# Eight weight tiles of a Trainium2 kernel begin at eight different places modulo 512 bytes

## The chip, the cores and the metric

The kernel runs on one core of a Trainium2 chip. A core has TensorE (matmuls, listed as PE, with its loads of the stationary operand as PEld), VectorE (DVE), ScalarE (ACT), GpSimd (POOL) and SyncE (SP, which only issues transfers here), an on-chip memory of 128 partitions from which these engines read (SBUF), the matmuls' accumulators (PSUM), and DMA queues between memory off the chip and SBUF. The metric is the device time of one execution in microseconds. A difference of 0.2% or more, some 2.2 us, can be told from no change.

## The reference, cut to what matters

Two layers of a transformer on a sequence of 512 with a width of 1024, in float32. Each layer projects the normalised input, runs two groups of attention heads, projects back, and then applies a dense network with a squared ReLU, whose hidden width is 4096:

```python
for l in range(DEPTH):
    h = rmsnorm(x, attn_norm[l])
    proj = jnp.einsum('bsd,de->bse', h, w_in[l])
    ...                        # stick-breaking heads and differential heads
    x = x + jnp.einsum('bse,ed->bsd', mixed, w_o[l])
    h = rmsnorm(x, mlp_norm[l])
    u = jnp.square(jax.nn.relu(jnp.einsum('bsd,df->bsf', h, w_ff1[l])))
    x = x + jnp.einsum('bsf,fd->bsd', u, w_ff2[l])
return rmsnorm(x, final_norm)
```

## The kernel before, in words

**Three products for one.** A matrix product in float32 is made of three matmuls on rounded operands. An operand a is split into hi, its rounding, and lo = a - hi, the rest; the helper `three` (lines 300, 301, 302) adds hi·hi, hi·lo and lo·hi in one accumulator. So every block of weights that arrives from memory is first split: ScalarE writes the rounded weights (`whi`, line 117, in `round`), VectorE writes the rest (`wlo`, line 133, in `split_part`).

**Units and turns.** All weights are cut into units of 128 partitions by 1024 elements (4096 bytes a partition), listed in `_UNITS` in the order in which TensorE uses them. The class `_Weights` loads, splits and hands out units. A pool named `wspl` holds two pairs of `whi` and `wlo` throughout; while the feed-forward stage of a layer runs, a second pool `f2` adds two more pairs. That makes the eight tiles. `spot` gives each unit its turn k (0 and 1 in `wspl`, 2 and 3 in `f2`), `owner` remembers which unit had the turn before, and `do_split` writes a unit's split into the program only behind the use of the unit that had its turn. Which of a pool's two buffers a tile gets is up to the pool: before the change `whi` and `wlo` are tags with two buffers each, and the tile framework, which also orders the instructions of each engine by its own planning, takes a buffer that is free.

**Where the split tiles are read.** In the attention stage a projection's unit is TensorE's loaded operand (`block`), or its streamed one (`values_of`, `all_values`), in matmuls of 512 or 256 columns. In the feed-forward stage the first product of a layer's first group is done by eight blocks of 24 matmuls with 512 columns (tiles named f); the other groups' first products are done by seven forms of 256 columns (`quad_group`, units of the kind s), and the second products by seven forms of 512 columns, in which the split weights stream and the activations Ah and Al are loaded (units of the kind f, into accumulators X, V, W and Y).

**Sources.** A unit's float32 weights arrive by transfers from SyncE in one of three `raw` buffers (`load`, line 110), in a tile of the feed-forward stage named q, waves, norms or first_a to first_c, some of them with a second transfer from GpSimd that adds another block on the way. A raw buffer is loaded again when its unit has been split; transfers of one queue keep their order.

**Places.** Before the change all eight tiles begin at multiples of 512 bytes in their partition, and so do the activations, the sources and the other large tiles. A few small ones and the two tiles named C of the stick-breaking heads, which begin at 352 and 384 modulo 512, don't. Matmuls read slices that begin at multiples of 512 bytes within their tiles.

Of the kernel before, what the change touches and what calls it, by code (L numbers as in the profile page):

```python
# [9 lines left out]
F32 = mybir.dt.float32  # L10
F32R = mybir.dt.float32r
# [6 lines left out]
P = 128  # L18
# [18 lines left out]
MAN = ()  # L37
APART = (("s", 0, 1), ("s", 3, 0), ("s", 3, 1))
_CTX = {}
DLY_R, DLY_D, DLY_S, DLY_Q = 3.5, 10.2, 9.0, 6.0  # L40
TAIL, ATT, DENSE, CAP = 6.0, 53.0, 145.0, 0.1
FORMS = ("11", "x3", "x2", "21", "x1", "x4", "22")
# [51 lines left out]
class _Weights:  # L94
# [24 lines left out]
    def split_part(self, i, a, b):  # L119
        nc = self.nc  # L120
        if i not in self.tiles and i in self.home:
            self.tiles[i] = self.home[i]
        if i not in self.tiles:
            k = self.spot(i)
            self.owner[k] = i
            self.turn = k + 1
            hi = self.pools[k // 2].tile([P, 1024], F32R, tag="whi", name=f"whi{i}")
            lo = self.pools[k // 2].tile([P, 1024], F32R, tag="wlo", name=f"wlo{i}")
            self.tiles[i] = (hi, lo)
        hi, lo = self.tiles[i]  # L130
        raw = self.first if (i, b) == (0, P) else self.raw[i]
        h = self.round(hi[:, a:b], raw[:, a:b])
        self.last = h, nc.vector.tensor_tensor(  # L133
            out=lo[:, a:b], in0=raw[:, a:b], in1=hi[:, a:b].bitcast(F32), op=ALU.subtract)

    def spot(self, i):
        n = 2 * len(self.pools) if _UNITS[i][0] in "1fs" else 2
        return self.turn % n if self.turn < n else 0
# [27 lines left out]
def trunk(ctx, tc, opened, xT, w, w2, w1, gfin, lamv, cos, sin, out):  # L166
    nc = tc.nc
    cp = ctx.enter_context(tc.tile_pool(name="cp", bufs=1))
    wraw = ctx.enter_context(tc.tile_pool(name="wraw", bufs=3))
    wspl = ctx.enter_context(tc.tile_pool(name="wspl", bufs=2))  # L170
    ps = ctx.enter_context(tc.tile_pool(name="ps", bufs=2, space=PSUM))
    dp = ctx.enter_context(tc.tile_pool(name="dp", bufs=1, space=bass.MemoryType.DRAM))

# [4 lines left out]
    def bank(tag, name):  # L178
        if tag == "any":
            tag = ("mm", "s", "s", "mm", "s")[turn[0] % 5]  # L180
            turn[0] += 1
        ring[0] += tag == "s"
        return ps.tile([P, 512], F32, tag=tag, name=name, bufs=banks[tag])

    if MAN:
        ctx.enter_context(tc.manual_schedule(engines={getattr(mybir.EngineType, e) for e in MAN}))
    W = _Weights(nc, w, wraw, wspl)
    cp.tile([P, 32], F32, tag="lead", name="lead")
    begin = cp.tile([P, 192], F32, tag="begin", name="begin")
    g_all, W.first = begin[:, 0:64], begin[:, 64:192]  # L190
    x = cp.tile([P, KC, S], F32, tag="x", name="x")
# [13 lines left out]
    for c in range(KC):  # L205
        nc.sync.dma_start(x[:, c, :], xT[c])
        if c % 2 == 0:
            for i in range(c < 4, 2):
                nc.sync.dma_start(raws[i][:, c * P : (c + 2) * P], w[i][:, c * P : (c + 2) * P])
    W.raw = dict(enumerate(raws))  # L210
    W.loaded = 2
    W.load(3)

# [51 lines left out]

    W.behind = behind

# [42 lines left out]
    def block(name, tag="mm"):  # L310
        pt = bank(tag, name)
        u = W.next("px" if name[0] == "p" else "1")
        for c in range(KC):
# [22 lines left out]
    for l in range(L):  # L336
# [539 lines left out]
        with ExitStack() as fctx:  # L876
            fe = fctx.enter_context(tc.tile_pool(name=f"fe{l}", bufs=1))
            fp = fctx.enter_context(tc.tile_pool(name=f"ff{l}", bufs=1))
            f2 = fctx.enter_context(tc.tile_pool(name=f"f2{l}", bufs=2))
            last = l == L - 1  # L880
            y = {q: (fe if q == (0, 0) else fp).tile([P, 2, 512], F32, tag=f"y{q[0]}{q[1]}", name=f"y{q[0]}{q[1]}_{l}")
                 for q in ((0, 0), (1, 0), (0, 1), (1, 1))}
            def quad(g, q, c):
                return w2[((l * GROUPS + g) * GP // 2 + c) * len(QUADS) + QUADS.index(q)]
# [7 lines left out]
            def fetch(g, form, c):  # L892
                t = W.raw[_INDEX[("f", l, g, form, c)]] = kept[(HOME[form], c)]
                nc.sync.dma_start(t, quad(g, "12" if form == "x3" else form, c))
                if form == "x3":
                    nc.gpsimd.dma_start(t, quad(g, "22", c), accum_op=ALU.add)
# [76 lines left out]
                            then(("f", l, g, "22", c), fetch, g + 1, "21", c)  # L973
            for c in range(GP // 2):
                fetch(0, "11", c)
            W.pools.append(f2)

            if not last:
# [229 lines left out]
            for g in range(GROUPS):  # L1208
# [24 lines left out]
                for form in FORMS2:  # L1233
# [20 lines left out]
                    for n, (c, i, r, part) in enumerate(work):  # L1254
# [3 lines left out]
                        hi, lo = (e[:, :, i, :] for e in sides[c])  # L1258
# [138 lines left out]
```

## Time and profile before

| what | before |
|---|---|
| device time, median of 3 runs | 1121.34 us (1121.09 to 1122.08) |
| profiled execution, device time | 1120.46 us |
| profiled execution, span from first to last instruction | 1118.7 us |
| mean granted TensorE clock | 0.998 |
| TensorE busy | 1111.2 us, 6345 matmuls |
| VectorE busy | 908.3 us |
| ScalarE busy | 689.7 us |
| GpSimd busy | 151.8 us |

The busy times are those of one profiled execution, in which the engines run side by side. A matmul's listed length goes beyond the start of the next, so the distance between starts says how fast TensorE gets on. In the view of stretches each column gives an engine's busy time in the stretch and, in brackets, the number of its instructions. In a group's row the number behind the bar is the group's total, then the mean of one instruction in ns, then the engine's idle time just before, with what ended it.

### The profile page before, as it was taken

Reading aid. Unit: us, or ns where it says so; the run is one execution under the profiler, and the core shown is the slowest. Engines: PE = TensorE matmul, PEld = TensorE weight load, DVE = VectorE, ACT = ScalarE, POOL = GpSimd, SP = SyncE. Lnnn points to the kernel's source line nnn. Section 1 sums busy time; section 2 is a strip of 40 time slices with the busy share of each in tenths; the row PEclk is TensorE's granted clock in tenths of the full one; section 3 lists DMA queues with packets and bytes.
Section 4 is the critical chain, followed back from the end, with each engine's and each line's share of the span. In section 5 each row is a group of like instructions: output and inputs, shape, how many; then the busy total and the mean of one; then the engine's idle time right before and its main releaser. Section 6 shows DMA issues by size and latency. Waiting matters only on the chain.

```text
span 1118.7 us, 17170 instructions
## 1 busy us (share of the span) xinstructions
PE 1111.2 (99%) x6345; PEld 973.8 (87%) x6345; DVE 908.3 (81%) x1333; ACT 689.7 (62%) x1131; POOL 151.8 (14%) x233
## 2 busy tenths in 40 slices
PE   9999999999999999999999999999999999999997
PEld 7889889888899899899878898988888998998986
DVE  7799788898668779779877897897787787797787
ACT  6447767577558457367344576775774584674665
POOL 1001343101001001001000014430011010010010
PEclk9999999999999999999999999999999999999999
DMA  7476353268787678648325654512677886687462
GB/s 256 131 189 187 114 135 110 78 233 218 179 213 183 176 189 189 190 131 213 108 76 152 188 161 128 164 58 76 210 178 184 201 189 177 182 186 207 114 132 95
DMA packets 61044, 181.25 MB, mean 162 GB/s; under 512 B 7456, under 2 KB 8736, under 8 KB 60960
## 3 DMA queue, kind: packets, MB, share of 16 engines
q1 hardware_dynamic: 50160, 141.84, 40.2%
q0 software_dynamic: 10368, 37.75, 19.4%
q8 instruction: 50, 0.82, 0.3%
q10 hardware_dynamic: 432, 0.56, 0.1%
q14 instruction: 34, 0.28, 0.1%
HBM read 150.77 MB, written 4.19 MB: 139 GB/s over the span
## 4 chain that ended last, share of the span: by engine, by line
PE 97%; DVE 1%; issue 1%; ACT 0%; DMA 0%; POOL 0%; POOLq 0%; DVEq 0%; ACTq 0%
PE X L300 9%; PE X L302 9%; PE X L301 9%; PE V L300 4%; PE V L302 4%; PE V L301 4%; PE wo L300 3%; PE wo L301 3%; PE wo L302 3%; PE f L302 3%; PE f L300 3%; PE f L301 3%; PE Y L302 2%; PE Y L300 2%; PE Y L301 2%; PE W L302 1%
## 5 line engine op out<-in xcount | busy, mean ns | idle before, releaser
L117 ACT ACTIVATE whi<-q 128x1024 fp32r<-128x1024 f32 x96 | 101.7, 1059 | 108.5 <-PE X L302 38.0
L133 DVE TENSOR_TENSOR wlo<-q,whi 128x1024 fp32r<-128x1024 f32 x96 | 117.3, 1223 | 46.7 <-ACT whi L117 46.5
L133 DVE TENSOR_TENSOR wlo<-raw,whi 128x1024 fp32r<-128x1024 f32 (+1 forms) x82 | 96.8, 1187 | 6.7 <-ACT whi L117 6.4
L117 ACT ACTIVATE whi<-raw 128x1024 fp32r<-128x1024 f32 (+1 forms) x82 | 80.9, 994 | 33.6 <-issue 17.9
L300 PE MATMUL X<-whi,Ah 128*128 128x512 f32 x248 | 97.7, 394 | 0.0
L301 PE MATMUL X<-wlo,Ah 128*128 128x512 f32 x248 | 96.8, 390 | 0.0
L302 PE MATMUL X<-whi,Al 128*128 128x512 f32 x248 | 96.8, 390 | 0.0
L133 DVE TENSOR_TENSOR wlo<-waves,whi 128x1024 fp32r<-128x1024 f32 x40 | 48.9, 1223 | 16.6 <-ACT whi L117 16.5
L117 ACT ACTIVATE whi<-waves 128x1024 fp32r<-128x1024 f32 x40 | 42.2, 1055 | 29.9 <-PE X L302 18.9
L300 PEld LDWEIGHTS X<-whi,Ah 128*128 128x128 f32 x248 | 46.6, 188 | 11.9 <-DVE y L1121 1.9
L302 PEld LDWEIGHTS X<-whi,Al 128*128 128x128 f32 x248 | 46.6, 188 | 9.8
L300 PE MATMUL X<-hxh,whi 128*128 128x256 f32 x192 | 54.5, 284 | 0.0
L302 PE MATMUL X<-hxh,wlo 128*128 128x256 f32 x192 | 54.4, 284 | 0.0
L302 PE MATMUL X<-h_hi,wlo 128*128 128x256 f32 x192 | 54.4, 284 | 0.0
L301 PE MATMUL X<-h_lo,whi 128*128 128x256 f32 x192 | 54.4, 284 | 0.0
L301 PE MATMUL X<-hxl,whi 128*128 128x256 f32 x192 | 54.4, 284 | 0.0
L301 PEld LDWEIGHTS X<-wlo,Ah 128*128 128x128 f32 x248 | 46.6, 188 | 8.9
L300 PE MATMUL X<-h_hi,whi 128*128 128x256 f32 x192 | 54.4, 283 | 0.0
L300 PE MATMUL f<-h_hi,whi 128*128 128x512 f32 x128 | 50.4, 394 | 0.0
L302 PE MATMUL f<-h_hi,wlo 128*128 128x512 f32 x128 | 50.0, 390 | 0.0
L301 PE MATMUL f<-h_lo,whi 128*128 128x512 f32 x128 | 49.9, 390 | 0.0
L240 DVE TENSOR_TENSOR Al<-x,Ah 128x512 fp32r<-128x512 f32 (+1 forms) x60 | 46.6, 793 | 3.7 <-ACT Ah L239 3.5
(764 smaller groups left out, 3705.4 us busy)
## 6 DMA issues: line engine op xcount, KB each, us to landing
raw<-in_w SPq DMA_DIRECT2D x78, 512.0 KB, 3.6
q<-in_w SPq DMA_DIRECT2D x48, 512.0 KB, 4.4
q<-in_w POOLq DMA_DIRECT2D x48, 512.0 KB, 7.5
waves<-in_w SPq DMA_DIRECT2D x28, 512.0 KB, 4.5
first_a<-in_w SPq DMA_DIRECT2D x12, 512.0 KB, 5.1
first_b<-in_w SPq DMA_DIRECT2D x12, 512.0 KB, 5.3
first_c<-in_w SPq DMA_DIRECT2D x12, 512.0 KB, 4.5
first_b<-in_w POOLq DMA_DIRECT2D x12, 512.0 KB, 6.2
```

The source lines that it names most:

```text
L117: return self.nc.scalar.activation(o, src, AF.Copy)
L133: self.last = h, nc.vector.tensor_tensor(out=lo[:, a:b], in0=raw[:, a:b], in1=hi[:, a:b].bitcast(F32), op=ALU.subtract)
L240: nc.vector.tensor_tensor(out=lo, in0=src, in1=hi.bitcast(F32), op=ALU.subtract)
L300: nc.tensor.matmul(pt, ah, bh, start=first, stop=False, skip_group_check=goes_on),
L301: nc.tensor.matmul(pt, ah, bl, start=False, stop=False, skip_group_check=goes_on),
L302: nc.tensor.matmul(pt, al, bh, start=False, stop=last, skip_group_check=goes_on))
```

## The change

The two buffers of each tag become two tags of one buffer each (`whi0`, `whi1`, `wlo0`, `wlo1`), and a tile takes the one that its turn names. A new function lays out a pool once, when it is opened: it allocates a pad, then a tile, four times, so that the tags stand in the pool in this order with these pads in between; neither the pads nor these first tiles are ever written or read. The first pool's pads sum to 512 bytes; the second pool's sum to 448, and it is the last in its stage. The eight tiles then begin, modulo 512, at 0 and 64 (`whi`, `wlo` of turn 0), 128 and 256 (turn 1), 192 and 320 (turn 2), 384 and 448 (turn 3).

```diff
+PADS = ((0, 64, 64, 128, 256), (192, 128, 64, 64))
...
-            hi = self.pools[k // 2].tile([P, 1024], F32R, tag="whi", name=f"whi{i}")
-            lo = self.pools[k // 2].tile([P, 1024], F32R, tag="wlo", name=f"wlo{i}")
+            hi, lo = (self.half(self.pools[k // 2], n, k % 2, f"{n}{i}") for n in ("whi", "wlo"))
...
+    def half(self, pool, kind, k, name):
+        return pool.tile([P, 1024], F32R, tag=f"{kind}{k}", name=name)
+
+    def lay_out(self, pool, pads):
+        places = [(k, kind) for k in range(2) for kind in ("whi", "wlo")]
+        for n, pad in enumerate(pads):
+            if pad:
+                pool.tile([P, pad // 4], F32, tag=f"pad{n}", name=f"pad{n}")
+            if n < 4:
+                k, kind = places[n]
+                self.half(pool, kind, k, f"place{kind}{k}")
...
-    wspl = ctx.enter_context(tc.tile_pool(name="wspl", bufs=2))
+    wspl = ctx.enter_context(tc.tile_pool(name="wspl", bufs=1))
...
     W = _Weights(nc, w, wraw, wspl)
+    W.lay_out(wspl, PADS[0])
...
-            f2 = fctx.enter_context(tc.tile_pool(name=f"f2{l}", bufs=2))
+            f2 = fctx.enter_context(tc.tile_pool(name=f"f2{l}", bufs=1))
...
+            W.lay_out(f2, PADS[1])
             W.pools.append(f2)
```

## The prediction

> **What bounds the kernel now.** I read the page's totals and the chain that ended last, then the busy time by stretch, then TensorE's order of time in single stretches.
>
> ```profile
> span 1118.7 us, 17170 instructions
> PE 1111.2 (99%) x6345; PEld 973.8 (87%) x6345; DVE 908.3 (81%) x1333; ACT 689.7 (62%) x1131; POOL 151.8 (14%) x233
> PE 97%; DVE 1%; issue 1%; ACT 0%; DMA 0%; POOL 0%; POOLq 0%; DVEq 0%; ACTq 0%
> ```
>
> ```profile
> core 0: us, PE busy (x) PEld busy (x) DVE busy (x) ACT busy (x) POOL busy (x), PEclk, DMA share, GB/s
> 0.00:224.00 224.00, 222.57 (x1208) 190.55 (x1209) 185.92 (x351) 139.55 (x297) 44.08 (x82) 1.00 0.51 150
> 246.00:532.00 286.00, 286.00 (x1734) 256.73 (x1733) 225.32 (x266) 180.86 (x231) 31.73 (x36) 1.00 0.75 192
> ```
>
> TensorE holds 97% of the chain. In the feed-forward stretch (246 to 532 us) it is busy for all 286.00 us at the full granted clock, so a faster or slower split shows only if TensorE has to wait for it, or if TensorE's own reading changes. A matmul's listed duration overlaps the next one; what counts is the distance between starts:
>
> ```profile
> 173.77 0.28 PE L438 MATMUL p0u<-whi,h_hi 128*128 128x256 f32 x1
> ...
> 175.19 0.28 PE L440 MATMUL p0u<-whi,h_lo 128*128 128x256 f32 x1
> ...
> 314.62 0.39 PE L300 MATMUL X<-whi,Ah 128*128 128x512 f32 x1
> ...
> 318.02 0.39 PE L300 MATMUL X<-whi,Ah 128*128 128x512 f32 x1
> ...
> 324.82 0.28 PE L300 MATMUL X<-hxh,whi 128*128 128x256 f32 x1
> ...
> 326.98 0.28 PE L300 MATMUL X<-hxh,whi 128*128 128x256 f32 x1
> ```
>
> From 314.62 to 318.02 there are 15 steps of 512 columns: 226.7 ns each. From 324.82 to 326.98 there are 18 steps of 256 columns: 120.0 ns each. The difference, 106.7 ns for 256 columns, is 0.417 ns a column, and extrapolated to no columns 13.3 ns are left in every step. The rounded weights are the streamed operand in the first stretch and the loaded one in the second, and both leave the same 13.3 ns. In the attention stretch from 173.77 to 175.19 there are 12 steps of 256 columns: 118.3 ns each, a fixed part of 11.7 ns.
>
> **The change, part by part.** Before, every one of the eight tiles (and every large tile) begins at a multiple of 512 bytes. After, whi and wlo of the first pool lie at 0 and 64, then 128 and 256; those of the second at 192 and 320, then 384 and 448.
>
> *Pads and placing tiles.* They are allocated and never written or read: no instruction, no DMA, 0 us. The first pool grows by 512 bytes, so what follows keeps its place modulo 512, and the second pool is the last of its stage. No DMA writes or reads the eight tiles, so transfers keep their places too.
>
> *The splits.* Each unit is rounded on ScalarE (L117) and its rest is taken on VectorE (L133), whose operands now begin at three different places.
>
> ```profile
> L133 DVE TENSOR_TENSOR wlo<-q,whi 128x1024 fp32r<-128x1024 f32 x96 | 117.3, 1223 | 46.7 <-ACT whi L117 46.5
> L117 ACT ACTIVATE whi<-q 128x1024 fp32r<-128x1024 f32 x96 | 101.7, 1059 | 108.5 <-PE X L302 38.0 <-PE V L302 24.7 <-PE Y L302 16.6
> L984 DVE TENSOR_TENSOR x<-x 128x512 f32<-128x512 f32 x48 | 33.1, 689 | 10.2 <-ACT x L1083 9.7
> L984 DVE TENSOR_TENSOR norms<-norms 128x256 f32<-128x256 f32 x16 | 6.8, 422 | 0.1
> L737 POOL TENSOR_TENSOR os<-os,rb 128x512 f32<-128x512 f32 x8 | 10.3, 1289 | 13.5 <-ACT rb L294 13.5
> L578 POOL TENSOR_TENSOR sig0s<-sig0s,C0s 128x512 f32<-128x512 f32 x8 | 9.2, 1146 | 13.3 <-DVE C0s L575 7.7 <-DVE sig0s L571 3.3 <-ACT turned L239 2.3
> ```
>
> VectorE's two-input operation takes 422, 689 and 1223 ns for 256, 512 and 1024 elements: 1.04 ns an element between each pair, a straight line with no extra as it gets longer. The nearest rows with another place are GpSimd's: os and rb both begin at multiples of 512 and take 1289 ns; sig does too, but C begins at 352 or 384 and is read one element further, and the same product takes 1146 ns, 143 ns less. So a place can matter to some engine. Carried over to 1024 elements that is 286 ns a split, the bound on either side. VectorE's own straight line speaks against a gain, so I take 0. At the bound a loss would hardly show either: the feed-forward stretch has units of 12 matmuls (2.72 us), VectorE is busy for 225.32 / 286.00 of that, 2.14 us, and 2.43 us after. Only where the chain leaves TensorE, at the end, does a split stand on it:
>
> ```profile
> 1099.94 1.07 ACT whi L117
> 1101.03 1.23 DVE wlo L133
> 1104.15 1.22 DVE wlo L133
> ```
>
> Two rests at 286 ns are 0.6 us, either way.
>
> *TensorE's reads.* 5388 of the 6345 matmuls (counted in the compiled kernel before) read one of the eight tiles. Half of 1056 such reads of whi in the attention stages and a quarter of 2536 in the feed-forward stages are of the one that stays at place 0; 4226 read a moved one. The only rows of before with an operand off the common place are the transposes that spread a column (rc, at 224 or 256), beside transposes at the common place:
>
> ```profile
> 131.84 0.49 PE L651 MATMUL T0s<-edge,sig0s 128*128 128x128 f32 x3
> 132.16 0.60 PE L293 MATMUL rb_d<-edge,rc 128*128 128x128 f32 x4
> ```
>
> The three starts from 131.84 to 132.16 are 107 ns apart, and the group of four lists 0.60 us where the group of three lists 0.49: one more transpose, 0.11 us more. No difference by place is seen: I take 0. The bounds: the whole fixed part could go, 4226 x 13.3 ns = 56 us; or it moves by what the attention stretch shows it can, 13.3 to 11.7, 1.6 ns x 4226 = 6.8 us, in either direction.
>
> The Trainium skill ("TensorE: Matmul & The Clock Gate", section Back-to-back issue gap) gives a gap of N/2.4 + 2.5 ns at full clock, 215.8 ns for 512 columns and 109.2 for 256. The trace has 226.7 and 120.0, 10.8 to 10.9 more; if the page's gap were the true floor and the surplus all collision, 4226 x 10.8 ns = 46 us would go and the sum would be 1075 us, an estimate from that page. Its page "SBUF — State Buffer" (section Who interferes with whom) says instead that TensorE's two read ports wait on nobody, by which the sum stays; the equal 13.3 ns at both widths, whichever operand is the split tile, agrees.
>
> *Each tile bound to its turn.* The pool gave a unit whichever of its two buffers was free first; now the turn decides. Followed through all units this alters one thing a layer: the fourth block of the first feed-forward product. Its split, the row at 242.91, used the buffer of the first block. Bound to turn 1 it shares with the second block, whose matmuls end at 247.8. This is an added wait of some 5 us.
>
> ```profile
> 242.91 1.05 ACT L117 ACTIVATE whi<-raw 128x1024 fp32r<-128x1024 f32 x1
> 249.17 1.05 ACT L239 ACTIVATE hxh<-x 128x1024 fp32r<-128x1024 f32 x1
> 251.16 1.04 ACT L117 ACTIVATE whi<-raw 128x1024 fp32r<-128x1024 f32 x1
> 250.45 1.22 DVE L240 TENSOR_TENSOR hxl<-x,hxh 128x1024 fp32r<-128x1024 f32 x1
> 251.58 1.28 DVE L240 TENSOR_TENSOR Al<-waves,Ah 128x512 fp32r<-128x512 f32 x2
> 247.57 0.39 PE L302 MATMUL f<-h_hi,wlo 128*128 128x512 f32 x1
> 253.24 0.39 PE L300 MATMUL f<-h_hi,whi 128*128 128x512 f32 x1
> 253.69 0.39 PE L302 MATMUL f<-h_hi,wlo 128*128 128x512 f32 x1
> 243.70 3.34 SPq L110 DMA_DIRECT2D raw<-in_w  x3
> 247.09 1.56 SPq L894 DMA_DIRECT2D q<-in_w  x3
> q<-in_w SPq DMA_DIRECT2D x5, 512.0 KB, 6.6
> q<-in_w POOLq DMA_DIRECT2D x2, 512.0 KB, 9.7
> 274.97 1.06 ACT L117 ACTIVATE whi<-q 128x1024 fp32r<-128x1024 f32 x1
> ```
>
> The block starts at 253.24 and needs its rest at 253.69. Rounding at 249.17 (the first place on ScalarE after the second block's eviction) ends at 250.22, the rest 1.22 us later at 251.4: early by 2.2 us, hidden behind the third block. Behind it on SyncE stand the raw load into the split's source buffer and the q loads of 247.09: from 251.4 they land 6.6 us and, with GpSimd's adding load, another 9.7 us later, at 267.7, and the split that reads them runs at 274.97. Cost 0.
>
> **Sum.** 1120.46 us (profiled execution: span 1118.7 and 1.76 around it) + 0 + 0 + 0 = 1120.5; the median shown, 1121.34, is 0.9 higher, and I give the forecast on that: 1121.3.
>
> **The rivals.** *The fixed part is partly a collision of the weight load with the stream, which different places loosen.* For it: the fixed part is not the same in all stretches (11.7 against 13.3), and GpSimd's two rows. Against: 13.3 ns at both widths and in both roles. By the 1.6 ns it gives 1121.3 - 6.8 = 1114.5; if all went, 1065. The skill's gap, above, is this rival's page.
>
> *The fourth block's split comes late (slower).* If its rounding lands only at 251.16 and its rest stands behind hxl and Al as well (VectorE is busy from 247 to 253 without a gap), it ends at 252.2 + 1.22 + 1.28 + 1.22 = 255.9, 2.2 us after 253.69, in both layers: 1125.7. It decides from the moment when the rest ends after 253.69. For it: VectorE is full there. Against: the split stands ahead of most of that work in program order.
>
> *The new places cost TensorE*, the first rival with its sign turned: 1128.1. Only the spread of the fixed part speaks for it, and the transposes against it.
>
> *The change doesn't do what it says* can only mean that places do not matter; that is the forecast.
>
> **How the numbers follow.** About 0.2% (2.2 us) is what a measurement of this kernel can tell from no change. Forecast: 0.55, its own range 1119.5 to 1123. First rival 0.21, most of it at 1114.5 and at most 0.06 of it below 1111. Late split 0.12, new places costing 0.12. Faster is the first rival, 0.21; slower the two others, 0.24. From 1111 to 1129 all is held but 0.06 below and some 0.06 above, of the costing places at more than the row's 1.6 ns.
>
> **What would show it.** Right: starts stay 226.7 and 120.0 ns apart in the same feed-forward stretches, L133 stays at 1223 and L117 at 1059 ns, the third rounding of the group at 241 to 245 us moves behind 247.9 and no matmul waits at 253. Wrong: another distance between starts for some turns and not for others (first or third rival, by sign), L133 off 1223 by more than 10 ns with the chain leaving TensorE more often, or a gap of TensorE before the fourth block. The prediction as a whole fails if the order of instructions on TensorE or VectorE comes out different far from that block, since I have assumed that it stays.

## The result and the profile after

Before, the time was 1121.21 us in the runs beside the changed kernel (1120.69 to 1122.08). After the change it is **1127.03 us** (1126.45 to 1127.36), a ratio of 1.0051 with a 95% interval of 1.0033 to 1.0068. The kernel became slower by 5.8 us, where no change was forecast. Lines 300 to 302 (`three`) are now 313 to 315, and line 117 is 118.

The page of the changed kernel, its totals and the chain:

```profile
span 1125.4 us, 17171 instructions
PE 1118.0 (99%) x6345; PEld 970.0 (86%) x6345; DVE 909.2 (81%) x1333; ACT 689.3 (61%) x1131; POOL 151.8 (13%) x233
PE 99%; issue 0%; DVE 0%; POOL 0%; ACT 0%; POOLq 0%; DVEq 0%; ACTq 0%
```

TensorE's busy time grew by 6.8 us (1111.2 to 1118.0) and the span by 6.7. VectorE, ScalarE and GpSimd are within 1 us of before. So nothing new is waited for: the same 6345 matmuls take longer. The two stretches shown of before, now:

```profile
core 0: us, PE busy (x) PEld busy (x) DVE busy (x) ACT busy (x) POOL busy (x), PEclk, DMA share, GB/s
0.00:224.00 224.00, 222.63 (x1200) 189.57 (x1201) 184.38 (x348) 139.53 (x297) 44.07 (x82) 1.00 0.51 149
246.00:532.00 286.00, 286.00 (x1729) 253.65 (x1728) 224.23 (x265) 180.64 (x232) 31.70 (x36) 1.00 0.75 192
```

In the same 224 us TensorE gets 1200 matmuls done instead of 1208, and 1729 instead of 1734 in the 286 us of the feed-forward stretch, at an unchanged granted clock of 1.00. In order of time, with the same kinds of steps as before:

```profile
317.76 0.39 PE L313 MATMUL X<-whi,Ah 128*128 128x512 f32 x1
...
321.22 0.39 PE L313 MATMUL X<-whi,Ah 128*128 128x512 f32 x1
...
328.27 0.28 PE L313 MATMUL X<-hxh,whi 128*128 128x256 f32 x1
...
330.06 0.28 PE L313 MATMUL X<-hxh,whi 128*128 128x256 f32 x1
```

Between the first two rows lie 15 steps of 512 columns, 230.7 ns each (226.7 before). Between the last two lie 15 steps of 256 columns, 119.3 ns each (120.0 before). The wide steps became longer and the narrow ones shorter. Whole stages show it best, because a stage's length divided by its matmuls is the step. The three rows are the eight blocks of the first product in layer 0 (192 matmuls, wide, split tile loaded), the second product of its second group (168, wide, split tile streamed) and the forms of its third group (336, narrow, split tile loaded). Each window goes from the first start of a stage to that of the next; the number in brackets counts a few neighbours too. Before:

```profile
core 0: us, PE busy (x), PEclk, DMA share, GB/s
236.44:280.44 44.00, 44.00 (x198) 1.00 0.84 233
359.02:397.42 38.40, 38.40 (x171) 1.00 0.74 185
397.42:437.73 40.31, 40.31 (x337) 1.00 0.76 189
```

After:

```profile
238.54:283.61 45.07, 45.07 (x197) 1.00 0.82 226
362.31:401.32 39.01, 39.01 (x171) 1.00 0.76 187
401.32:441.02 39.70, 39.70 (x337) 1.00 0.75 187
```

The blocks take 1.07 us more, the second product 0.61 more, and the forms 0.61 **less**. Over the whole execution I added up the distances between starts by kind of matmul. Kinds are told apart by which tile a matmul reads:

| us between starts, summed | before | after | wide only | forms at 64 | all at 64 | forms at 88 |
|---|---|---|---|---|---|---|
| 512 columns, with a split tile (2964) | 682.0 | 692.9 | 692.5 | 683.6 | 692.3 | 683.0 |
| forms of 256 columns (2016) | 241.9 | 238.2 | 241.8 | 237.4 | 233.0 | 228.6 |
| all other matmuls (1365) | 187.2 | 186.6 | 186.5 | 187.0 | 185.7 | 186.9 |
| total | 1111.0 | 1117.8 | 1120.8 | 1108.0 | 1111.0 | 1098.5 |

After the change there are two terms of opposite sign, +10.9 us and -3.7 us. The -0.6 us of the others is no more than sums of steps left alone differ by: the wide steps come to 682.0, 683.0 and 683.6 us in three kernels in which all of them are at 0. The last four columns belong to the experiments.

### The profile page after: what moved, and what is told of

Read it like the earlier page. It is cut to its first block, busy times and chain, and to the rows that moved or that the text cites. A ratio compares the mean times of both kernels' runs of the same rounds, so it can differ in the third digit from the quotient of the medians.

```text
span 1125.4 us, 17171 instructions
## 1 busy us (share of the span) xinstructions
PE 1118.0 (99%) x6345; PEld 970.0 (86%) x6345; DVE 909.2 (81%) x1333; ACT 689.3 (61%) x1131; POOL 151.8 (13%) x233
## 4 chain that ended last, share of the span: by engine, by line
PE 99%; issue 0%; DVE 0%; POOL 0%; ACT 0%; POOLq 0%; DVEq 0%; ACTq 0%
PE X L313 9%; PE X L315 9%; PE X L314 9%; PE V L315 4%; PE V L313 4%; PE V L314 4%; PE wo L315 3%; PE f L315 3%; PE f L314 3%; PE wo L314 3%; PE f L313 3%; PE wo L313 3%; PE Y L314 2%; PE Y L315 2%; PE Y L313 2%; PE W L315 1%
## 5 line engine op out<-in xcount | busy, mean ns | idle before, releaser
L118 ACT ACTIVATE whi<-q 128x1024 fp32r<-128x1024 f32 x96 | 101.6, 1059 | 108.4 <-PE X L315 40.5
L133 DVE TENSOR_TENSOR wlo<-q,whi 128x1024 fp32r<-128x1024 f32 x96 | 117.2, 1222 | 47.6 <-ACT whi L118 47.5
L133 DVE TENSOR_TENSOR wlo<-waves,whi 128x1024 fp32r<-128x1024 f32 x40 | 48.9, 1222 | 16.8 <-ACT whi L118 16.8
```

The lines of the kernel that those rows point to most:

```text
L118: return self.nc.scalar.activation(o, src, AF.Copy)
L133: self.last = h, nc.vector.tensor_tensor(out=lo[:, a:b], in0=raw[:, a:b], in1=hi[:, a:b].bitcast(F32), op=ALU.subtract)
```

## The experiments

Three theories stood at the start. The first, *relative place*: a step depends on how far apart the loaded and the streamed operand begin. The second, *changing places*: it costs that the place differs from matmul to matmul. The third, *binding*: the fixed turns or a changed order cost.

**The binding alone.** All pads are 0, while the tags, the turns and the first pool with one buffer a tag stay.

```diff
-PADS = ((0, 64, 64, 128, 256), (192, 128, 64, 64))
+PADS = ((0, 0, 0, 0, 0), (0, 0, 0, 0))
```

> The change without its pads: each tile is bound to its turn and the tiles stand in the new order, but all eight begin at multiples of 512 bytes again. If the places cost the time (theory 1 and 2), this runs as before, 1121 us within 2 us, with steps of 226.7 ns (512 columns) and 120.0 ns (256 columns) in the feed-forward stretch. If the binding or the new order of the tiles costs it (theory 3), it runs near 1127 us and the steps of 512 columns are 230 ns and more.

Measured: 1121.1 us, ratio 1.000 (0.999 to 1.0009). Its stages, in the same order:

```profile
237.37:281.37 44.00, 44.00 (x197) 1.00 0.83 234
359.95:398.34 38.39, 38.39 (x171) 1.00 0.75 188
398.34:438.65 40.31, 40.31 (x337) 1.00 0.76 189
```

These are the lengths of before within 0.01 us. The binding costs nothing, and the whole difference is in the places.

**All eight at one place, and the rests at another.** Only the pads differ:

```diff
+PADS = ((256, 0, 0, 0, 256), (256, 0, 0, 0))       # all at 256
+PADS = ((64, 0, 0, 0, 448), (64, 0, 0, 0))         # all at 64
+PADS = ((0, 256, 256, 256, 256), (0, 256, 256, 256))   # whi at 0, wlo at 256
```

> All eight tiles at one place, 256 modulo 512; their partners in the matmul stay at 0. Theory 1, what matters is the place of the loaded operand against that of the streamed one: every step that reads a split tile is off, so steps of 512 columns average 231 to 232 ns, those of 256 columns 118, and the time is 1127 us or a little more. Theory 2, what costs is that the places change from matmul to matmul: with one place for all, steps are even again, 226.7 and 120.0 ns, and the time is 1121 us. Theory 3 (binding): 1127 us whatever the steps.

> All eight tiles at place 64. Theory 1 as for place 256 (512 columns at 231 to 232 ns, 256 columns near 118, 1127 us), though the amount may depend on the place. Theory 2: 1121 us, even steps of 226.7 and 120.0 ns.

> The rounded weights at 0, the rests at 256. Theory 1: two of three matmuls of a product keep equal places and one does not, so the loss is about a third of that at 256 for all, 1123 us, and the steps that read a rest are the long ones. Theory 2: places change within every product, so it is as slow as the change, 1127 us, and the steps that read rounded weights are long too.

All at 256: 1121.13 us, ratio 0.9999. Rests at 256: 1121.22, ratio 1.0001. So 256 is the same place as 0, and two places that alternate cost nothing if they are 256 apart. The first theory had expected 1127 and 1123 us here; it can only stand with places taken modulo 256. All at 64 gave a median of 1118.57 us (ratio 0.9979, 0.9968 to 0.999), and its ten executions lie far apart, from 1116.23 to 1121.37. Here no place changes from matmul to matmul, and yet the wide steps grew by about as much as after the change (692.3 and 692.9 us in the table). So the loss does not need changing places; whether changing places has a part of its own beside that is taken up with the finer scans. Two stages of forms of this kernel, which do the same work at the same place:

```profile
399.37:437.47 38.10, 38.10 (x337) 1.00 0.76 191
476.15:515.72 39.57, 39.57 (x337) 1.00 0.63 174
```

The first goes at 113.4 ns a step, the second at 117.8. One place can have two lengths. Three of the six form stages took the one and three the other in this execution, and each that changes sides moves the time by 1.5 us; this would account for the spread of 5.1 us, though only this execution was traced.

The wide steps can have two lengths too. The first 96 matmuls of the second product in the first and in the second group of layer 0, in the same execution:

```profile
283.57:305.97 22.40, 22.40 (x97) 1.00 0.69 177
360.69:382.67 21.98, 21.98 (x99) 1.00 0.73 163
```

The same work at the same place takes 233.3 ns a step in the first stretch and 228.9 in the second; layer 1 repeats both.

**Everything shifted together.** This separates a distance between operands from a place as such. Before's first small tile is 64 bytes longer, so all tiles in the memory begin 64 bytes further on.

```diff
-    cp.tile([P, 32], F32, tag="lead", name="lead")
+    cp.tile([P, 48], F32, tag="lead", name="lead")
```

> The first small tile is 64 bytes longer, so that all tiles in the memory, split tiles and activations alike, begin 64 bytes further on; order and everything else as before. Relative-place theory (the distance between the loaded and the streamed operand's places counts): steps stay at 227.1 and 120.0 ns and the time at 1121.2 us. Rival (the place of each operand by itself counts): the steps change as with all eight at 64, to 229 to 233 ns and 113 to 118 ns, or further, since now both operands lie at 64; the time moves by more than 2 us either way.

Measured: 1121.35 us, ratio 1.0002 (0.9992 to 1.0012). The stages of blocks, second product and forms:

```profile
237.18:281.18 44.00, 44.00 (x198) 1.00 0.87 235
359.76:398.14 38.38, 38.38 (x170) 1.00 0.77 186
398.14:438.46 40.32, 40.32 (x338) 1.00 0.73 187
```

All as before, although every split tile lies at 64 now. So no tile's place counts by itself, only where tiles lie relative to each other. This run moves everything and does not say which two have to be compared. Accesses of the other engines can be set aside by the traces: the steps of the forms of before average 119.99 ns while VectorE is busy and 120.02 while it is not, and 120.0 with ScalarE busy or not. Nor does a stage's length follow the transfers: in the run with only the forms at 64, below, two stages of forms have 39.58 us at DMA shares of 0.76 and 0.63. That leaves what TensorE reads and writes itself, most likely the loaded and the streamed operand.

**A place for each unit.** From here on the kernel before is used with tiles 256 bytes longer, in which a unit takes a slice that begins where `place` says (modulo 256). Turns and order are those of before.

```diff
-            hi = self.pools[k // 2].tile([P, 1024], F32R, tag="whi", name=f"whi{i}")
-            lo = self.pools[k // 2].tile([P, 1024], F32R, tag="wlo", name=f"wlo{i}")
+            at = place(_UNITS[i]) // 4
+            hi, lo = (self.pools[k // 2].tile([P, 1088], F32R, tag=n, name=f"{n}{i}")[:, at : at + 1024]
+                      for n in ("whi", "wlo"))
```

*A scan.*

> One kernel with a different place for each stage: whi and wlo of the second to fourth group's forms (256 columns, split tile loaded) begin at 16, 32, 64 (layer 0) and 96, 128, 192 (layer 1) modulo 256; those of the second products (512 columns, split tile streamed) at 16, 32, 64, 96 (layer 0) and 128, 160, 192, 224 (layer 1); the eight blocks of the first product (512 columns, split tile loaded) at 0, 32, ... 224; all other units at 0. Relative-place theory with a period of 256: at 64 the forms take 113.3 to 117.8 ns a step and the second products about 229, as with all eight at 64; at 128 something else than at 0. Period of 128: the stages at 128 take 120.0 and 227.1 as at 0, and 192 repeats 64, 160 repeats 32, 224 repeats 96. If only the lowest places matter (16 and 32 already differ from 0 as 64 does), all stages but those at 0 look like 64. Rival (neighbours carry it: a step's length follows from the irregularity of the stage before, not from its own place): the stages do not sort by place, and the same place in two stages gives two different means. Time: between 1113 and 1127 us, only the steps by stage count.

Measured in one execution: 1124.21 us. The mean steps in ns, without the few of over 260 where one stage hands over to the next:

| place | 0 | 16 | 32 | 64 | 96 | 128 | 160 | 192 | 224 |
|---|---|---|---|---|---|---|---|---|---|
| blocks (512, loaded; layer 0) | 227.0 | | 232.5 | 233.2 | 234.0 | 232.2 | 233.4 | 229.3 | 233.1 |
| second product (512, streamed) | | 231.7 | 233.4 | 229.1 | 233.4 | 233.0 | 234.1 | 233.4 | 233.2 |
| forms (256, loaded) | | 118.3 | 118.4 | 113.4 | 117.3 | 118.7 | | 117.8 | |

A period of 128 is out: at 128 the steps are not those at 0. A streamed tile at 64 gives 229.1 and a loaded tile at 192 gives 229.3; both mean that the streamed operand begins 64 further on than the loaded one, modulo 256. The other way round, 192 streamed and 64 loaded, it is 233.4 and 233.2. This fits the relative place, now in two stages with exchanged roles; it is no proof, since a streamed tile at 64 was also seen at 233.3 (above). No wide stage is as short as at distance 0; every stage of forms is shorter than the 120.0 there.

*Only the forms, at 64* (`place` gives 64 for units of the kind s, otherwise 0):

> Only the units of the forms with 256 columns (groups two to four, split tile loaded) begin at 64 modulo 256; every other unit at 0, in the same eight tiles, each 256 bytes longer. Relative-place theory: the 2016 steps of these forms shorten from 120.0 ns to between 113.3 and 117.8, a gain of 4.4 to 13.5 us, and the 512-column steps stay at 227.1: 1107.6 to 1116.7 us. Rival (the shorter steps with all eight at 64 came from the disturbed 512-column neighbours): the forms stay near 120.0 and the time at 1121.2.

Measured: 1116.82 us, ratio 0.9963 (0.995 to 0.9977). The second product and the forms of the third and fourth group:

```profile
359.58:397.96 38.38, 38.38 (x170) 1.00 0.76 191
397.96:437.54 39.58, 39.58 (x338) 1.00 0.76 190
475.92:515.50 39.58, 39.58 (x338) 1.00 0.63 175
```

The forms gain 0.73 us a stage while the wide stage keeps its 38.38. All six form stages of the profiled execution go at 117.8 ns, at the slow end of the range; the time lies 0.1 us beyond the range that was expected.

*Only the wide ones, at the places of after* (units of the kind s at 0, all others where their turn puts them after the change):

> Each unit's split tiles begin, modulo 256, where its turn puts them after the change (0 and 64, 128 and 0, 192 and 64, 128 and 192), except the units of the forms with 256 columns, which begin at 0. Theory (the change is two terms of opposite sign, by relative place modulo 256): the 512-column steps lengthen as after the change, +11.0 us in all, and the forms stay at 120.0 ns: 1121.1 + 11.0 = 1132 us, slower than after the change. Rival (the shorter 256-column steps after the change only followed from irregular neighbours): the forms shorten here too although they lie at 0, and the time is that of after, 1127. Rival (period 512, so that places 256 apart are not the same): 512-column steps other than after.

Measured: 1130.41 us, ratio 1.0085 (1.0068 to 1.0101), 1.6 us less than expected. Its blocks, second product and forms:

```profile
237.92:282.99 45.07, 45.07 (x198) 1.00 0.82 227
362.28:401.28 39.00, 39.00 (x170) 1.00 0.73 185
401.29:441.59 40.30, 40.30 (x338) 1.00 0.76 187
```

The wide stages have the lengths of after, 45.07 and 39.00; the forms that of before, 40.30. So the two terms are separate, and neither follows from irregular stages next to it. Some tiles lie 256 bytes from where they lie after the change, and the lengths are the same, as a period of 256 wants it.

*Finer scans of the forms and of the second product:*

> Only the units of the forms with 256 columns move, whi and wlo alike, one place for each half of a group: 40, 48, 56, 72, 80, 88 (layer 0), 8, 24, 60, 68, 104, 232 (layer 1); all other units at 0. If what counts is in which 64 bytes the operand begins, 72, 80, 88 and 104 give 117.8 as 64 did and 8 to 60 do not; if every 4 bytes count, the step changes gradually from place to place. If a step has few preferred lengths that the predecessors choose between (113.3 and 117.8 were both seen at 64), some halves come out at 113.3. Time 1113 to 1121 us, only the steps by half count.

> Only the units of the second products (512 columns, split tile streamed) move, one pair of places (whi, wlo) for each of 16 parts: both alike at 8, 48, 56, 72, 80, 240; or apart: 64 and 0, 0 and 64, 64 and 128, 64 and 192, 128 and 192, 128 and 64, 32 and 96, 0 and 128, 192 and 64, 0 and 192; all other units at 0. Relative-place theory: no part is shorter than the 226.7 ns at 0, those at 64 from the loaded tile take 229, the rest up to 234. If a place exists at which 512 columns take fewer than 226.7, it shows here. Time 1123 to 1129 us, only the steps by part count.

The scan of the forms took 1116.86 us in one execution. Steps by half group: 119.1 at 40, 118.3 at 48, 117.8 at 56, 118.3 at 72, 118.7 at 80, 113.4 at 88, 115.6 at 8, 121.9 at 24, 119.5 at 60, 118.4 at 68, 117.8 at 104 and at 232. It is no matter of 64-byte pieces alone, since 72, 80 and 88 differ, and not gradual either. The halves at 24 and 60 include steps of 130 ns and more and say less. The second product's scan took 1126.56 us: its 16 parts lie between 227.1 (both at 240) and 235.1 ns (both at 72), with whi and wlo apart no better than alike. No wide part fell below the 226.7 of distance 0.

Four of the parts with whi and wlo apart have one of the two at 0, and they show that a matmul's own distance does not set its step alone. With whi at 64 and wlo at 0, 96 steps:

```profile
519.04:541.45 22.41, 22.41 (x99) 1.00 0.69 175
```

These are 233.4 ns each; the 32 that stream wlo, at distance 0, are the longer ones with 235.6, against 232.2 for the 64 that stream whi. With whi at 0 and wlo at 64 the steps of whi are 232.5 ns, not 226.7. The changed kernel shows the same: the 288 steps of its second products at distance 0 average 232.2 ns, and the 576 steps of its forms at distance 0 average 117.7 instead of 120.0. So in a mixture of places the matmuls around a step count too, and the relative-place theory holds as it was put only where a whole stage has one place, and even there 64 allows two lengths. How much of the +10.9 us is distance and how much is mixture stays open.

*Does 88 always give the short step?*

> Again only the units of the 256-column forms move, all others lie at 0. Layer 0: second group all at 88; third group its first unit at 80 and the rest at 88; fourth group its first half at 80 and its second at 88, as in the scan of the forms. Layer 1: second group all at 8; third group its first half at 12 and its second at 8; fourth group its first half at 4 and its second at 88. Theory that a place alone sets the step: 113.4 ns wherever 88 is, 115.6 wherever 8 is. Theory that the units before choose between several lengths which a place allows: the fourth group of layer 0 repeats 118.7 and 113.4, and at least one of the other stretches at 88 or 8 comes out at another length than 113.4 or 115.6. Time 1110 to 1116 us, only the steps count.

One execution took 1111.52 us. Three of its form stages: all at 88; the first unit at 80 and the rest at 88; all at 8:

```profile
319.48:357.58 38.10, 38.10 (x337) 1.00 0.75 190
395.94:434.15 38.21, 38.21 (x338) 1.00 0.74 191
871.59:910.42 38.83, 38.83 (x337) 1.00 0.75 193
```

The step at 88 came out at 113.3 behind a wide stage, behind units at 80 and behind units at 4; at 8 it was 115.6 behind a wide stage and behind units at 12; 80 repeated its 118.7. At these places the units before choose nothing. What chooses at 64 stays open: ten executions of one kernel, with the same units before, spread over 5.1 us. Hence the last run, with all units of the forms at 88 and everything else at 0:

```diff
+def place(unit, k):
+    return (88, 88) if unit[0] == "s" else (0, 0)
```

> All units of the 256-column forms at 88 modulo 256, everything else at 0. If 88 gives 113.3 ns whatever came before, as in its four stretches so far, 2016 steps gain 6.65 ns each: 13.4 us, 1121.2 - 13.4 = 1107.8 us, with the 512-column steps at 227.1. If the units before can still choose another length, some groups stay near 118 and the time lies between 1108 and 1117, with executions apart by some 1.5 us for each group, as with all eight at 64. If the splits or transfers can't keep up with the shorter steps, TensorE waits ahead of single forms and part of the 13.4 us is lost there.

Measured: **1107.88 us** (1107.40 to 1108.47), ratio 0.9884 (0.9867 to 0.99), faster than both kernels. Its page and its blocks, second product and forms:

```profile
span 1106.2 us, 17170 instructions
PE 1098.5 (99%) x6345; PEld 959.9 (87%) x6345; DVE 907.2 (82%) x1333; ACT 688.5 (62%) x1131; POOL 151.9 (14%) x233
```

```profile
236.97:280.97 44.00, 44.00 (x198) 1.00 0.86 234
357.33:395.70 38.37, 38.37 (x170) 1.00 0.80 195
395.70:433.80 38.10, 38.10 (x337) 1.00 0.77 192
```

The forms take 38.10 us instead of 40.31 in all six stages, 13.3 us together, and waits of TensorE grow by no more than 0.3 us.

## Why the prediction was wrong, point by point

**What bounds the kernel**: right. TensorE holds 99% of the chain after, and only its own reading could move the time.

**Pads, and the binding to a turn**: right at 0; the pads of size 0 with the binding kept give 1121.1 us. The fourth block's split moved as foreseen, in the views by order of time of ScalarE, VectorE and TensorE after the change:

```profile
250.09 1.06 ACT L118 ACTIVATE whi<-raw 128x1024 fp32r<-128x1024 f32 x1 [3.29 <-PE f L314]
251.18 1.22 DVE L133 TENSOR_TENSOR wlo<-raw,whi 128x1024 fp32r<-128x1024 f32 x1 [0.32 <-ACT whi L118]
255.72 0.40 PE L313 MATMUL f<-h_hi,whi 128*128 128x512 f32 x1
256.19 0.39 PE L315 MATMUL f<-h_hi,wlo 128*128 128x512 f32 x1
```

The rest is there at 252.40, 3.8 us ahead of the matmul that reads it (2.2 were forecast). The rival of the late split fell here: VectorE put this rest ahead of hxl.

**The splits**: right at 0. GpSimd's 143 ns did not carry over; with three operands at different places the groups are unchanged to 1 ns:

```profile
L118 ACT ACTIVATE whi<-q 128x1024 fp32r<-128x1024 f32 x96 | 101.6, 1059 | 108.4 <-PE X L315 40.5
L133 DVE TENSOR_TENSOR wlo<-q,whi 128x1024 fp32r<-128x1024 f32 x96 | 117.2, 1222 | 47.6 <-ACT whi L118 47.5
```

**TensorE's reads: the step that failed.** I took 0, with bounds of 6.8 us either way from the spread of the fixed part, and of 56 us for all of it. Measured are +10.9 us over 2964 wide steps (3.7 ns each), -3.7 us over 2016 forms (1.8 ns each) and -0.6 us elsewhere, which is within the scatter. Two readings led there. The first was the nearest row: transposes of 128 columns, one with an operand off the common place, both at 107 ns. They read neither at the widths in question nor with the split tiles, and at 107 ns they are far above the 66.7 ns that 0.417 ns a column and 13.3 ns would give 128 columns (an estimate from the rows of the prediction), so they could not show the effect. The second was the equal 13.3 ns at both widths and in both roles, read as a sign that nothing collides. But all those rows had one thing in common, both operands at distance 0, and so they could not say what another distance does. That holds for the 1.6 ns of the bounds as well: 118.3 and 120.0 ns both come from distance 0, and their difference is no effect of place. In the forms at 88 the same fixed part is 113.3 - 106.7 = 6.6 ns, half of it.

The Trainium skill's "SBUF — State Buffer" (section Who interferes with whom), on which the zero leaned beside this, says that TensorE's two read ports are independent and that TensorE waits on nobody. As to the other engines the traces agree, since the steps are the same whether VectorE is busy or not (119.99 and 120.02 ns). The zero did not follow from it, for the same matmuls take 120.0 or 113.3 ns by where their operands lie; whether the two ports meet is not shown. The Trainium skill's "TensorE: Matmul & The Clock Gate" (section Back-to-back issue gap) has 109.2 and 215.8 ns, by a formula that it gives for an isolated matmul; the shortest lasting steps of these runs are 113.3 and 226.7.

**The rivals.** That new places cost TensorE, with a chance of 0.12, had the direction right: 1128.1 forecast against 1127.03. Its size was luck: 1.6 ns on each of 4226 reads stood for two terms of opposite sign, and the 1.6 ns had nothing to do with place. The first rival, that different places shorten a step, is borne out for the forms alone; at the places of the change its 3.7 us were outweighed. That the two rivals' common cause, a collision of the weight load with the stream, is behind it was not shown. Putting a place where each width wants it, rather than where the turn falls, is what separates 1107.88 from 1127.03 us.

**What stays open.** Why a distance lengthens a wide step and shortens a narrow one, and why 64 allows two lengths and 88 one, is not settled, nor how the places of successive matmuls act together. That the load of the next operand and the stream of the present one meet in the memory would fit a distance with a period of 256 bytes, but no run measures the two reads by themselves. The rows of the weight loads say a little. In these stages a load begins 2 to 5 ns after the start of the matmul before its own. A group of loads in the third group's forms, before and with the forms at 88:

```profile
L300 PEld LDWEIGHTS X<-hxh,whi 128*128 128x128 f32 x32 | 6.2, 192 | 0.0
L304 PEld LDWEIGHTS X<-hxh,whi 128*128 128x128 f32 x32 | 6.0, 188 | 0.0
```

In the forms the loads are listed 4 ns shorter where the step is 6.7 ns shorter. In the wide stages they average 187 to 189 ns at every place tried, whether the step is 227 or 235, so the longer wide steps don't show in the length of the loads.

## What to carry to other kernels

Where TensorE is the bound, divide a whole stage's length by its matmuls, for each width apart, and ask what all the rows that agree have in common: a constant that never varied proves nothing about its own effect. The place of the loaded operand relative to the streamed one is worth a scan, by slices of a slightly longer tile, with a place of its own for each kind of matmul in one run. Keep the place alike within a stage, since a mixture also slowed matmuls that lay at 0. Sum an effect by kinds before trusting its sign, because +10.9 and -3.7 us look like a small loss.

## What the runs showed of the hardware that I had not expected

- In these fp32r matmuls, where each has a load of its own, the step depends on where the loaded and the streamed operand lie relative to each other modulo 256 bytes. With the activations at 0 and a stage's split tiles all at one place: 256 columns (split tile loaded) take 120.0 ns at 0, 113.3 at 88, 115.6 at 8, and 113.4 or 117.8 at 64; 512 columns take 226.7 at 0, 227.1 at 240, and 229 to 235 at the other places tried.
- Where places are mixed within a stage, a matmul at distance 0 does not keep its step: 232.2 ns instead of 226.7 in the second products after the change, 117.7 instead of 120.0 in the forms.
- With the split tiles at 64 the forms hold one of two steps through a whole stage of 336 matmuls, and which one varies between stages and executions (1116.23 to 1121.37 us). The wide steps have two lengths there as well, 228.9 and 233.3 ns. At 88 all eleven stretches seen, half a stage or longer, were at 113.3 to 113.4.
- ScalarE's and VectorE's splits keep their 1059 and 1222 ns, within 2 ns, at all places tried (1057 and 1221 with the forms at 88).
